# A two-layer decoder trunk on one core: the first norm's gain spread by TensorE from one row, the weight splits put behind the norm, the small S5 parameters moved by one block

## The chip, the cores and the metric

The kernel runs on one core of a Trainium2 chip. The metric is the device time of one execution in microseconds (us). In the text PE is TensorE, DVE VectorE, ACT ScalarE, POOL GpSimd, and SP the engine that issues most DMA transfers (SyncE).

## What is computed

256 tokens of width 1024 go through two layers. The part that matters here is the start of the first layer: a root-mean-square norm, then a gated feed-forward block.

```python
def rmsnorm(x, g):
    xf = x.astype(jnp.float32)
    y = xf * lax.rsqrt(jnp.mean(xf * xf, axis=-1, keepdims=True) + RMS_EPS)
    return (y * g.astype(jnp.float32)).astype(x.dtype)

def swiglu(x, w_gate, w_up, w_down):
    return (jax.nn.silu(x @ w_gate) * (x @ w_up)) @ w_down

for l in range(DEPTH):
    x = x + 0.5 * swiglu(rmsnorm(x, ffn1_norm[l]), ffn1_gate[l], ffn1_up[l], ffn1_down[l])
    ...
```

Behind it, in each layer, stand a mixer with three branches (sparse attention, an S5 state-space layer, dilated attention) and a second feed-forward block. The S5 layer needs tables that are made from its parameters (`s5_lam_re`, `s5_lam_im`, `s5_log_dt` and others). They are made while the first feed-forward block runs.

## The kernel before

Tokens stand in two tiles of 128, `x[0]` and `x[1]`. The weights arrive in units of 512 KB (`load_unit`, L210), four buffers deep (`raw`). Each unit is split in two: ACT copies it in a rounded form to `wh` (L221), and DVE makes the remainder `wl` (L228); in the first layer's feed-forward part DVE does nearly all of these remainders. Five pairs of `wh` and `wl` are held. A product of the kernel is three matmuls, high by high, high by low and low by high (`mm3`, L106 to L108), so a unit needs 24 matmuls of 256 columns in the gate and up parts. The hidden width of 2816 is worked off in blocks j of 256; a block takes two units for the gate and two for the up weights, and two for the down weights of block j-2.

The norm of a token tile (`norm_half`, L264, and `norm_tok`, L266 to L286) is a chain over the engines: ACT squares the two halves of the tile with a running sum, DVE adds the sums (L269), POOL raises to -1/2 (L271), DVE multiplies each half by that and by the gain (`xn`, L274), PE transposes it in four pieces (L278) into the PSUM tiles `y` and `p2`, ACT copies the result to the high part `hTh` (L282) and DVE makes the low part `hTl` (L283).

Before the first products PE runs 12 matmuls on zeros (`WARM`, L1147). The gain of the first norm is fetched by SP in two halves, each as one row of 2 KB read for all 128 partitions (L1150 and L1156), in between the loads of x[0] and of the first two weight units. So SP's first transfers are x[0], gain half, unit 0, gain half, unit 1, x[1], units 2 and 3, a table of masks (`cm`), and then the next units as their buffers come free.

The small parameters of the S5 layer are loaded in the feed-forward block's step j = 1 and worked on in step j = 2 (`step`, L1125 to L1138). They go by `setup_small`, which transposes `st_small` on PE into the PSUM tile `y` (L405) and copies it out on DVE (`smT`, L406), and by `setup_s5_params`, which transposes three more tiles into the same PSUM tile `y` (L438) and works on from there on DVE. `y` has one buffer, so L438 cannot start before L406 has read it.

The order of the instructions on each engine is set by a scheduler, which lays the program out by priorities and its own estimate of each operation's time. `tc.high_priority` raises a priority, and `tc.issue_after` (in `behind`, L288) makes an instruction stand behind another one.

Of the kernel before, what the change touches and what calls it, by code (L numbers as in the profile page):

```python
# [27 lines left out]
ALU = mybir.AluOpType  # L28
# [44 lines left out]
def _body(ctx, tc, nc, I, out, depth, dbg):  # L73
# [112 lines left out]
    WARM = 12  # L186
# [26 lines left out]
    def emit_unit(i):  # L213
        while pos[0] <= min(i + RB - 1, len(units) - 1):
            unit_t[pos[0]] = load_unit(pos[0])
            pos[0] += 1
        r = unit_t.pop(i)
        k, n = r.shape[1], r.shape[2]
        al, tags, nb = (tb, ("xh", "xl"), 4) if i in local else (sb, ("wh", "wl"), WB_)
        hv, lv = (al([P, 1024], F32R, tg, nb)[:, :k * n].rearrange("p (k c) -> p k c", k=k) for tg in tags)  # L220
        A.activation(hv, r, AF.Copy)  # L221
        if i in START or lo_share[0] and i % lo_share[1] < lo_share[0]:
            for c in range(0, n, n // 2):
                cs = slice(c, c + n // 2)
                G.tensor_tensor(lv[:, :, cs], r[:, :, cs], hv[:, :, cs].bitcast(F32), op=ALU.subtract)  # L225
        else:
            c = n - n * lo_share[2] // 8
            V.tensor_tensor(lv[:, :, :c], r[:, :, :c], hv[:, :, :c].bitcast(F32), op=ALU.subtract)  # L228
            if c < n:
                G.tensor_tensor(lv[:, :, c:], r[:, :, c:], hv[:, :, c:].bitcast(F32), op=ALU.subtract)  # L230
        unit_t[i] = (hv, lv)
# [33 lines left out]

    def norm_tok(t, g, h):  # L266
# [4 lines left out]
        G.tensor_tensor(rs, ms, mh[:, 0:1], op=ALU.pow)  # L271
        for q in range(2):
            xn = tb([P, 512], F32, "xn", 2)
            V.scalar_tensor_tensor(xn, x[t][:, q * 512:(q + 1) * 512], rs, g[:, q * 512:(q + 1) * 512],  # L274
                                   op0=ALU.mult, op1=ALU.mult)
            pt = ps(("y", "p2")[q])
# [5 lines left out]
            A.activation(hv, p3, AF.Copy)  # L282
# [842 lines left out]
    def step(gen, l):  # L1125
        def f(j):
# [4 lines left out]
            if j >= 2:  # L1131
                if l == 0 and j == 2:
# [7 lines left out]
    with Phase():  # L1140
        table(AF.Silu)
        with tc.high_priority():
# [3 lines left out]
            for _ in range(WARM):  # L1146
                PE.matmul(pw, wz[:, :P], wz, start=True, stop=True)  # L1147
            g = tb([P, D], F32, "G", 1)
            gs = I["ffn1_norm"][0].unsqueeze(0).broadcast_to([P, D])
            nc.sync.dma_start(g[:, :512], gs[:, :512])  # L1150
            for i in range(3):
# [3 lines left out]
                if i == 0:  # L1155
                    nc.sync.dma_start(g[:, 512:], gs[:, 512:])  # L1156
# [59 lines left out]
```

## Time and profile before

| | |
|---|---|
| runs | 1357.64, 1356.96 and 1354.83 us; median 1356.96 |
| the profiled execution | 1357.2 us |
| its span in the trace | 1355.4 us; 1.8 us lie around it |
| PE, share of the span | 98% |
| DVE, ACT, POOL | 61%, 52%, 34% |
| mean DMA rate | 196 GB/s |

A timeline row gives the start, the duration, the engine, the line, the operation, its output and inputs, how many equal ones follow, and in brackets for how long the engine had been idle and what ended that. Matmuls overlap on PE, so the step from one start to the next, not a matmul's own duration, is what it costs. A windows row gives the stretch, its length, the busy us (and the count of instructions) of PE, of PE's weight loads, of DVE, ACT and POOL, then the granted clock of PE (1.00 is 2.4 GHz, 0.50 is 1.2 GHz), the DMA share and GB/s.

### The profile page before, as it was taken

What the parts mean: (1) busy time and instruction counts of PE and PEld (TensorE: products, weight loads), DVE (VectorE), ACT (ScalarE), POOL (GpSimd) and SP (SyncE); (2) the same over time, 40 slices, a digit from 0 to 9 for tenths busy, and PEclk for the clock granted to TensorE, in tenths of its full rate; (3) what the DMA queues carried; (4) which work ended last, traced back from release to release, by engine and by line L of the source; (5) the groups of instructions that cost most, each with busy time, mean ns of one, the idle gap of its engine ahead of it and who ended that gap; (6) DMA issues with size and microseconds to landing.
All of it is one profiled execution on the core that took longest, in us unless ns stands there. A gap on an engine that the chain in (4) does not pass through costs nothing.

```text
span 1355.4 us, 25390 instructions
## 1 busy us (share of the span) xinstructions
PE 1331.6 (98%) x10120; PEld 1256.8 (93%) x10120; DVE 826.8 (61%) x1172; ACT 699.8 (52%) x1020; POOL 465.3 (34%) x333
## 2 busy tenths in 40 slices
PE   8999999999999999999999999999999999999998
PEld 7999988999999989999999999889999999899997
DVE  5696755996433665444675586569864337544443
ACT  5444445677644544444544444457766355544442
POOL 1442565454246531111122247254532555111110
PEclk9999999999999999999999999999999999999999
DMA  8866688666657556666756677766766576466662
GB/s 249 224 188 214 223 267 235 198 184 191 184 134 226 172 171 204 186 187 187 236 154 203 202 231 240 243 201 176 194 193 178 157 221 194 155 188 186 186 187 94
DMA packets 246326, 265.68 MB, mean 196 GB/s; under 512 B 51136, under 2 KB 224192, under 8 KB 246208
## 3 DMA queue, kind: packets, MB, share of 16 engines
q1 hardware_dynamic: 244400, 260.40, 64.7%
q10 hardware_dynamic: 1808, 3.67, 0.8%
q8 instruction: 79, 1.29, 0.4%
q14 instruction: 39, 0.32, 0.1%
HBM read 244.92 MB, written 18.58 MB: 194 GB/s over the span
## 4 chain that ended last, share of the span: by engine, by line
PE 76%; DVE 9%; DMA 7%; POOL 3%; ACT 2%; issue 2%; SPq 0%; ACTq 0%; DVEq 0%; POOLq 0%
PE mm L108 17%; PE mm L106 17%; PE mm L107 17%; PE pt L108 3%; PE pt L107 3%; PE pt L106 3%; DVE wl L228 3%; PE sc L108 3%; PE sc L107 3%; PE sc L106 3%; DMA raw<-in_w_in_dram 2%; DMA raw<-in_ffn_down_dram 1%; DMA raw<-in_ffn_gate_dram 1%; DMA raw<-in_ffn_up_dram 1%; PE pt L820 1%
## 5 line engine op out<-in xcount | busy, mean ns | idle before, releaser
L228 DVE TENSOR_TENSOR wl<-raw,wh 128x1024 fp32r<-128x1024 f32 (+3 forms) x376 | 443.5, 1186 | 340.8 <-ACT wh L221 327.2
L221 ACT ACTIVATE wh<-raw 128x1024 fp32r<-128x1024 f32 (+2 forms) x396 | 414.2, 1048 | 453.8 <-PE mm L107 240.8
L108 PE MATMUL mm<-hTh,wl 128*128 128x256 f32 x1728 | 490.7, 284 | 0.0
L107 PE MATMUL mm<-hTl,wh 128*128 128x256 f32 x1728 | 490.7, 284 | 0.0
L106 PE MATMUL mm<-hTh,wh 128*128 128x256 f32 x1728 | 489.0, 283 | 0.0
L106 PEld LDWEIGHTS mm<-hTh,wh 128*128 128x128 f32 x1728 | 326.5, 189 | 2.2
L108 PEld LDWEIGHTS mm<-hTh,wl 128*128 128x128 f32 x1728 | 325.9, 189 | 0.6 <-issue 0.3
L107 PEld LDWEIGHTS mm<-hTl,wh 128*128 128x128 f32 x1728 | 325.2, 188 | 1.3 <-issue 0.3
L371 POOL TENSOR_TENSOR al<-aa,ah 128x512 fp32r<-128x512 f32 x40 | 71.3, 1781 | 456.8 <-ACT ah L370 456.8
L230 POOL TENSOR_TENSOR wl<-raw,wh 128x384 fp32r<-128x384 f32 (+2 forms) x108 | 144.9, 1347 | 174.7 <-ACT wh L221 142.3
L106 PE MATMUL mm<-wh,hTh 128*128 128x256 f32 (+1 forms) x496 | 142.9, 290 | 0.0
L107 PE MATMUL mm<-wl,hTh 128*128 128x256 f32 (+1 forms) x496 | 141.8, 288 | 0.0
L108 PE MATMUL mm<-wh,hTl 128*128 128x256 f32 (+1 forms) x496 | 140.6, 288 | 0.0
L107 PEld LDWEIGHTS mm<-wl,hTh 128*128 128x128 f32 x496 | 94.1, 190 | 1.2 <-issue 0.3
L106 PEld LDWEIGHTS mm<-wh,hTh 128*128 128x128 f32 x496 | 94.0, 190 | 1.1 <-issue 0.3
L108 PEld LDWEIGHTS mm<-wh,hTl 128*128 128x128 f32 x496 | 93.1, 189 | 1.0 <-issue 0.3
L225 POOL TENSOR_TENSOR wl<-raw,wh 128x512 fp32r<-128x512 f32 x40 | 56.5, 1434 | 53.7 <-ACT wh L221 48.4
L107 PE MATMUL pt<-wl,ah 128*128 128x512 f32 x144 | 56.4, 392 | 0.0
L108 PE MATMUL pt<-wh,al 128*128 128x512 f32 x144 | 56.4, 391 | 0.0
L108 PE MATMUL sc<-wh,al 128*128 128x512 f32 x144 | 56.3, 391 | 0.0
L106 PE MATMUL pt<-wh,ah 128*128 128x512 f32 x144 | 56.2, 390 | 0.0
L107 PE MATMUL sc<-wl,ah 128*128 128x512 f32 x144 | 56.1, 390 | 0.0
(311 smaller groups left out, 2074.7 us busy)
## 6 DMA issues: line engine op xcount, KB each, us to landing
raw<-in_w_in_dram SPq DMA_DIRECT2D x100, 512.0 KB, 4.3
raw<-in_ffn_gate_dram SPq DMA_DIRECT2D x88, 512.0 KB, 4.4
raw<-in_ffn_up_dram SPq DMA_DIRECT2D x88, 512.0 KB, 4.7
raw<-in_ffn_down_dram SPq DMA_DIRECT2D x88, 512.0 KB, 4.3
raw<-in_w_out_dram SPq DMA_DIRECT2D x16, 512.0 KB, 4.2
Gd<-xh SPq DMA_DIRECT2D x8, 512.0 KB
Ad<-xl SPq DMA_DIRECT2D x8, 512.0 KB, 5.6
x<-Ad SPq DMA_DIRECT2D x8, 512.0 KB, 5.3
```

The lines of the kernel that those rows point to most:

```text
L106: PE.matmul(o, lh, rh, start=start, stop=False)
L107: PE.matmul(o, lh, rl, start=False, stop=False)
L108: PE.matmul(o, ll, rh, start=False, stop=stop)
L221: A.activation(hv, r, AF.Copy)
L225: G.tensor_tensor(lv[:, :, cs], r[:, :, cs], hv[:, :, cs].bitcast(F32), op=ALU.subtract)
L228: V.tensor_tensor(lv[:, :, :c], r[:, :, :c], hv[:, :, :c].bitcast(F32), op=ALU.subtract)
L230: G.tensor_tensor(lv[:, :, c:], r[:, :, c:], hv[:, :, c:].bitcast(F32), op=ALU.subtract)
L371: G.tensor_tensor(al, a, ah.bitcast(F32), op=ALU.subtract)
L820: PE.transpose(pt[:, i * P:(i + 1) * P], s[:, (b0 + i) * P:(b0 + i + 1) * P], ident)
```

## The change

Three things are done.

- The first norm's gain is fetched as one row of 4 KB to one partition, and two matmuls of that row with a column of ones spread it over 128 partitions in the PSUM tile `sc`. They stand between 7 and 5 of the zero matmuls. `xn` then reads the gain from PSUM.
- The split of unit 0 on DVE (`wl`) is put behind the last `xn` that was written (x[1]'s second half), and the split of unit 1 on ACT (`wh`) behind the last `hTh` (x[1]'s second). In `norm_tok` both `xn` are now written ahead of the transposes.
- The work on the small parameters moves from step j = 2 to j = 3.

```diff
-    WARM = 12
+    WARM = 7, 5
...
-        A.activation(hv, r, AF.Copy)
+        with behind(order.get("h") if i == 1 else None):
+            A.activation(hv, r, AF.Copy)
...
-            V.tensor_tensor(lv[:, :, :c], r[:, :, :c], hv[:, :, :c].bitcast(F32), op=ALU.subtract)
+            with behind(order.get("x") if i == 0 else None):
+                V.tensor_tensor(lv[:, :, :c], r[:, :, :c], hv[:, :, :c].bitcast(F32), op=ALU.subtract)
...
+        xns = []
         for q in range(2):
             xn = tb([P, 512], F32, "xn", 2)
-            V.scalar_tensor_tensor(xn, x[t][:, q * 512:(q + 1) * 512], rs, g[:, q * 512:(q + 1) * 512],
+            xns.append(xn)
+            order["x"] = V.scalar_tensor_tensor(xn, x[t][:, q * 512:(q + 1) * 512], rs, g[:, q * 512:(q + 1) * 512],
                                    op0=ALU.mult, op1=ALU.mult)
+        for q, xn in enumerate(xns):
...
-            A.activation(hv, p3, AF.Copy)
+            order["h"] = A.activation(hv, p3, AF.Copy)
...
-                if l == 0 and j == 2:
+                if l == 0 and j == 3:
...
-            for _ in range(WARM):
-                PE.matmul(pw, wz[:, :P], wz, start=True, stop=True)
-            g = tb([P, D], F32, "G", 1)
-            gs = I["ffn1_norm"][0].unsqueeze(0).broadcast_to([P, D])
-            nc.sync.dma_start(g[:, :512], gs[:, :512])
+            g1, one = tb([1, D], F32, "G1"), tb([1, P], F32, "one")
+            nc.sync.dma_start(g1, I["ffn1_norm"][0].unsqueeze(0))
+            V.memset(one, 1.0)
...
+            g = ps("sc")
+            w = warm(WARM[0])
+            for q in range(2):
+                with behind(w):
+                    w = PE.matmul(g[:, q * 512:(q + 1) * 512], one, g1[:, q * 512:(q + 1) * 512], start=True, stop=True)
+            with behind(w):
+                warm(WARM[1])
...
-                if i == 0:
-                    nc.sync.dma_start(g[:, 512:], gs[:, 512:])
```

**ACT at the start.** Of the names, `junk` are the squares of the norm, `x0` and `x1` the token tiles, `wh_48`, `wh_51` and so on the high parts of units 0, 1 and so on, and `hTh` the transposed norm's high part, twice for each token tile. Before:

```order
L264 ACTIVATE junk_23_122,n_ss_21_119<-x0_1_63 128x512
L221 ACTIVATE wh_48_187<-raw_18_111 128x1024
L282 ACTIVATE hTh_24_124<-y_29_132 128x4x128
L221 ACTIVATE wh_51_193<-raw_19_114 128x1024
L282 ACTIVATE hTh_24_124<-p2_31_141 128x4x128
L264 ACTIVATE junk_33_149,n_ss_32_148<-x1_2_64 128x512
L264 ACTIVATE junk_34_151,n_ss_32_148<-x1_2_64 128x512
L221 ACTIVATE wh_54_199<-raw_20_117 128x1024
L221 ACTIVATE wh_57_205<-raw_47_185 128x1024
L282 ACTIVATE hTh_24_124<-y_38_159 128x4x128
L245 DMA G_42_179<-in_mix_norm_dram 128x1024
L282 ACTIVATE hTh_24_124<-p2_40_168 128x4x128
L221 ACTIVATE wh_60_211<-raw_50_191 128x1024
```

and with the change, where units 0, 1, 2 and 3 are `wh_50`, `wh_53`, `wh_56` and `wh_59`:

```order
L266 ACTIVATE junk_25_126,n_ss_23_123<-x0_1_63 128x512
L222 ACTIVATE wh_50_191<-raw_20_116 128x1024
L266 ACTIVATE junk_35_153,n_ss_34_152<-x1_2_64 128x512
L289 ACTIVATE hTh_26_128<-y_32_138 128x4x128
L266 ACTIVATE junk_36_155,n_ss_34_152<-x1_2_64 128x512
L289 ACTIVATE hTh_26_128<-p2_33_145 128x4x128
L289 ACTIVATE hTh_26_128<-y_41_165 128x4x128
L247 DMA G_44_183<-in_mix_norm_dram 128x1024
L289 ACTIVATE hTh_26_128<-p2_42_172 128x4x128
L222 ACTIVATE wh_53_197<-raw_21_118 128x1024
L222 ACTIVATE wh_56_203<-raw_22_121 128x1024
L222 ACTIVATE wh_59_209<-raw_49_189 128x1024
```

Now x1's first square stands between unit 0 and the first `hTh` of x0, and units 1 and on stand behind all four `hTh`.

**DVE at the start.** `wl_49` and `wl_52` are the low parts of units 0 and 1. Before:

```order
L274 SCALAR_TENSOR_TENSOR xn_28_130<-x0_1_63,n_rs_27_128,G_17_109 128x512
L274 SCALAR_TENSOR_TENSOR xn_30_139<-x0_1_63,n_rs_27_128,G_17_109 128x512
L228 TENSOR_TENSOR wl_49_188<-raw_18_111,wh_48_187 128x1024
L283 TENSOR_TENSOR hTl_25_125<-y_29_132,hTh_24_124 128x4x128
L228 TENSOR_TENSOR wl_52_194<-raw_19_114,wh_51_193 128x1024
L283 TENSOR_TENSOR hTl_25_125<-p2_31_141,hTh_24_124 128x4x128
L269 TENSOR_SCALAR n_ms_35_153<-n_ss_32_148 128x1
L274 SCALAR_TENSOR_TENSOR xn_37_157<-x1_2_64,n_rs_36_155,G_17_109 128x512
L274 SCALAR_TENSOR_TENSOR xn_39_166<-x1_2_64,n_rs_36_155,G_17_109 128x512
L228 TENSOR_TENSOR wl_55_200<-raw_20_117,wh_54_199 128x1024
L408 TENSOR_TENSOR sgn_10_78<-cm_3_66 128x1 x2
L228 TENSOR_TENSOR wl_58_206<-raw_47_185,wh_57_205 128x1024
```

and with the change, where they are `wl_51` and `wl_54`:

```order
L280 SCALAR_TENSOR_TENSOR xn_30_134<-x0_1_63,n_rs_29_132,sc_19_101 128x512
L280 SCALAR_TENSOR_TENSOR xn_31_136<-x0_1_63,n_rs_29_132,sc_19_101 128x512
L290 TENSOR_TENSOR hTl_27_129<-y_32_138,hTh_26_128 128x4x128
L273 TENSOR_SCALAR n_ms_37_157<-n_ss_34_152 128x1
L290 TENSOR_TENSOR hTl_27_129<-p2_33_145,hTh_26_128 128x4x128
L280 SCALAR_TENSOR_TENSOR xn_39_161<-x1_2_64,n_rs_38_159,sc_19_101 128x512
L280 SCALAR_TENSOR_TENSOR xn_40_163<-x1_2_64,n_rs_38_159,sc_19_101 128x512
L230 TENSOR_TENSOR wl_51_192<-raw_20_116,wh_50_191 128x1024
L415 TENSOR_TENSOR sgn_10_78<-cm_3_66 128x1 x2
L290 TENSOR_TENSOR hTl_27_129<-y_41_165,hTh_26_128 128x4x128
L436 MEMSET sp_eb_153_850 128x64
L290 TENSOR_TENSOR hTl_27_129<-p2_42_172,hTh_26_128 128x4x128
L230 TENSOR_TENSOR wl_54_198<-raw_21_118,wh_53_197 128x1024
```

Unit 0's low part has gone from behind x0's `xn` to behind x1's, unit 1's behind the last `hTl`; the gain now comes from the PSUM tile `sc`.

**PE at the start, with the change.** After x0's transposes PE has one product, then x1's transposes, then eleven more products of unit 0 with x0, of which the last are here:

```order
L108 MATMUL mm_70_231<-wh_50_191,hTl_27_129 128x256
L106 MATMUL mm_70_231<-wh_50_191,hTh_26_128 128x256
L107 MATMUL mm_70_231<-wl_51_192,hTh_26_128 128x256
L108 MATMUL mm_70_231<-wh_50_191,hTl_27_129 128x256
L106 MATMUL mm_70_231<-wh_53_197,hTh_26_128 128x256
L106 MATMUL mm_71_232<-wh_56_203,hTh_26_128 128x256
L107 MATMUL mm_70_231<-wl_54_198,hTh_26_128 128x256
```

The products that follow unit 0's need unit 1's high part (`wh_53`), unit 2's (`wh_56`) and unit 1's low part (`wl_54`); the last row is the fifteenth product. Before, 25 products stood ahead of x1's transposes.

**DVE around the small parameters.** `smT` is the copy for which PE's second set of transposes waits. Before, `wl_102` and `wl_105` are the low parts of units 11 and 12:

```order
L228 TENSOR_TENSOR wl_91_439<-raw_79_344,wh_90_438 128x1024
L228 TENSOR_TENSOR wl_102_494<-raw_82_374,wh_101_493 128x1024
L369 TENSOR_TENSOR aa_77_342<-mm_85_405,silu_76_341 128x512
L228 TENSOR_TENSOR wl_105_524<-raw_86_406,wh_104_523 128x1024
L406 COPY smT_11_79<-y_119_652 128x8
L409 TENSOR_TENSOR gqk_12_80<-smT_11_79 128x2
L410 TENSOR_TENSOR gqk_12_80<-smT_11_79 128x2
```

and with the change, where `wl_120`, `wl_135` and `wl_138` are those of units 16, 17 and 18:

```order
L376 TENSOR_TENSOR aa_100_493<-mm_108_556,silu_99_492 128x512
L230 TENSOR_TENSOR wl_120_629<-raw_109_557,wh_119_628 128x1024
L230 TENSOR_TENSOR wl_135_685<-raw_112_587,wh_134_684 128x1024
L230 TENSOR_TENSOR wl_138_715<-raw_115_620,wh_137_714 128x1024
L413 COPY smT_11_79<-y_152_843 128x8
L416 TENSOR_TENSOR gqk_12_80<-smT_11_79 128x2
```

The copy has moved by one block of weights; in both orders it stands right behind the low part of a block's first down unit. A part of the mixer in the second layer stands in another order too; the rest of the program stands as before.

## Rows read from the trace of the kernel before

**Rows 1.** The page: the span, and busy time by engine.

```profile
span 1355.4 us, 25390 instructions
PE 1331.6 (98%) x10120; PEld 1256.8 (93%) x10120; DVE 826.8 (61%) x1172; ACT 699.8 (52%) x1020; POOL 465.3 (34%) x333
```

**Rows 2.** Waits of PE, whole span: for what, us in total, times, longest.

```profile
PE y L278 <- DVE xn L274: 4.0, 4, 1.1
...
PE y L438 <- DVE smT L406: 1.8, 1, 1.8
```

**Rows 3.** Timeline of PE: start, us, engine, line, operation, out<-in, count, idle before.

```profile
1.18 5.30 PE L1147 MATMUL mm<-warm 128*128 128x512 bf16 x12 [1.18 <-DVE mh L252]
...
10.59 0.56 PE L106 MATMUL mm<-wh,hTh 128*128 128x256 f32 x1
...
17.31 0.28 PE L108 MATMUL mm<-wh,hTl 128*128 128x256 f32 x1
...
18.03 0.28 PE L108 MATMUL mm<-wh,hTl 128*128 128x256 f32 x1
```

**Rows 4.** Windows: first products alone (PE, PEld, DVE, ACT), then all instructions.

```profile
10.58:17.30 6.72, 5.56 (x28) 4.71 (x29) 0.00 (x0) 0.00 (x0) 0.77 1.07 354
...
10.20:13.60 3.40, 3.38 (x15) 2.83 (x14) 3.29 (x5) 2.91 (x7) 0.00 (x0) 0.50 1.08 359
...
365.20:368.60 3.40, 3.40 (x18) 3.40 (x18) 1.19 (x3) 1.77 (x5) 0.00 (x0) 0.50 1.01 268
```

**Rows 5.** Timeline of ACT, first 18 us.

```profile
4.19 0.63 ACT L264 ACTIVATE junk<-x 128x512 bf16<-128x512 f32 x1 [1.50 <-DMA x<-in_x_dram]
...
10.65 1.06 ACT L221 ACTIVATE wh<-raw 128x1024 fp32r<-128x1024 f32 x1 [0.66 <-DMA raw<-in_ffn_gate_dram]
...
12.10 0.62 ACT L264 ACTIVATE junk<-x 128x512 bf16<-128x512 f32 x1
...
12.84 0.63 ACT L264 ACTIVATE junk<-x 128x512 bf16<-128x512 f32 x1
...
16.70 0.60 ACT L282 ACTIVATE hTh<-p 128x512 fp32r<-128x512 f32 x1
...
17.39 1.06 ACT L221 ACTIVATE wh<-raw 128x1024 fp32r<-128x1024 f32 x1
```

**Rows 6.** Timeline of DVE, 13 to 20 us.

```profile
13.60 0.22 DVE L269 TENSOR_SCALAR n_ms<-n_ss 128x1 f32<-128x1 f32 x1
...
14.48 1.42 DVE L274 SCALAR_TENSOR_TENSOR xn<-x,n_rs,G 128x512 f32<-128x512 f32 x2 [0.67 <-POOL n_rs L271]
...
15.81 1.22 DVE L228 TENSOR_TENSOR wl<-raw,wh 128x1024 fp32r<-128x1024 f32 x1
...
18.84 0.68 DVE L283 TENSOR_TENSOR hTl<-p,hTh 128x512 fp32r<-128x512 f32 x1
```

**Rows 7.** Windows of the start; the last two columns are DMA share and GB/s.

```profile
0.00:4.00 4.00, 2.82 (x7) 1.04 (x8) 0.30 (x2) 1.89 (x4) 0.69 (x6) 1.00 0.52 154
4.00:7.00 3.00, 2.48 (x6) 0.60 (x4) 0.43 (x2) 1.44 (x4) 0.56 (x1) 1.00 0.84 216
7.00:9.20 2.20, 0.66 (x4) 0.42 (x4) 0.57 (x2) 0.74 (x1) 0.00 (x0) 1.00 1.05 378
```

**Rows 8.** Timelines of SP, PE, ACT and DVE around 43 us, by time.

```profile
35.63 1.38 SPq L210 DMA_DIRECT2D raw<-in_ffn_down_dram  x1
...
40.24 0.22 PE L405 MATMUL y<-ident,st_small 8*128 8x8 f32 x1
...
42.54 1.06 ACT L221 ACTIVATE wh<-raw 128x1024 fp32r<-128x1024 f32 x1 [2.27 <-DMA raw<-in_ffn_down_dram]
...
43.63 1.23 DVE L228 TENSOR_TENSOR wl<-raw,wh 128x1024 fp32r<-128x1024 f32 x1 [1.50 <-ACT wh L221]
...
44.77 0.16 DVE L406 COPY smT<-y 128x8 f32<-128x8 f32 x1
...
44.99 0.34 PE L438 MATMUL y<-ident,sp_raw 64*128 64x64 f32 x2 [1.84 <-DVE smT L406]
```

More of the change, by code (lines that the diff above doesn't have):

```diff
@@ L264, in norm_half @@
         A.activation(jk, x[t][:, q * 512:(q + 1) * 512], AF.Square, scale=1.0 / 32, accum_out=ssq[t][:, q:q + 1])
+    order = {}
     def norm_tok(t, g, h):
@@ L1145, in _body, with warm @@
             pw = ps("mm")
-            for _ in range(WARM):
-                PE.matmul(pw, wz[:, :P], wz, start=True, stop=True)
-            g = tb([P, D], F32, "G", 1)
-            gs = I["ffn1_norm"][0].unsqueeze(0).broadcast_to([P, D])
-            nc.sync.dma_start(g[:, :512], gs[:, :512])
+            g1, one = tb([1, D], F32, "G1"), tb([1, P], F32, "one")
+            nc.sync.dma_start(g1, I["ffn1_norm"][0].unsqueeze(0))
+            V.memset(one, 1.0)
+            def warm(n):
+                for _ in range(n):
+                    w = PE.matmul(pw, wz[:, :P], wz, start=True, stop=True)
+                return w
+            g = ps("sc")
[5 more added lines that the diff above has]
+                warm(WARM[1])
             for i in range(3):
```

## The prediction, made before the changed kernel was run

> **What bounds the kernel now.** The page comes first [rows 1]: PE is busy for 1331.6 of 1355.4 us, DVE for 61%, ACT for 52%. With PE at 98% the time is PE's work plus the moments in which PE waits or runs at half clock, so a change can only win or lose those. The waits of PE are the second view [rows 2]: four waits for a norm's `xn`, 4.0 us together, and one of 1.8 us for `smT`, the copy of the small parameters. The timelines of PE, ACT and DVE at the start come third [rows 3, 5, 6], since two of the three edits lie there. Last are the rows around 43 us [rows 8], where the third edit lies.
>
> At the start, read how far PE has come once the norm of both token tiles is behind it. From 17.31 us on PE starts a product every 0.12 us (six steps to 18.03 [rows 3]). By 17.30 it has done 28 products since 10.59 [rows 3, 4], the first of them at half clock (0.50 from 10.2 to 13.6 [rows 4]). 28 x 0.12 = 3.4 us, so PE stands where it would stand had it begun at 13.9 us without a pause. That number is what the change has to beat.
>
> **The start, first half: when x[1] lands.** The gain's two broadcast halves (0.52 MB written) go, and a row of 4 KB comes. With the change ACT's order is unit 0's split, the first square of x1, only then the first `hTh` of x0. So everything behind hangs on the landing of x1, L. Before, 2.10 MB went ahead of x1: x0, two gain halves, two units. The windows add up to 4.0 x 154 + 3.0 x 216 + 2.2 x 378 = 2.10 MB by 9.2 us [rows 7], and the last of these, unit 1, is taken up by ACT at 10.65 [rows 5], 1.4 us later. Now 2.10 MB is the whole of x0, units 0 and 1, and x1 itself. At the old rates x1 lands at 9.2 + 1.4 = 10.6: the upper bound. The lower one takes the slow stretch from 4 to 7 us (216 GB/s) as the gain's doing: 0.62 MB are over by 4.0, the other 1.48 MB go at 378, so at 7.9, and x0's delay is added (its 0.52 MB are through at 3.4 by the first of these rates, and ACT takes it up at 4.19 [rows 5]): 8.7. Nothing before tells these apart; I take about the middle, **L = 9.5**.
>
> **The start, second half: the chain from L.** First square at L; to the next ACT instruction 0.74 (12.10 to 12.84 [rows 5]); one `hTh` of 0.60 [rows 5] in between; second square at L + 1.34. Its `hTh` follows at +0.74 and takes 0.60, so L + 2.68; DVE makes `hTl` from it, 0.68 [rows 6], until L + 3.36. POOL's root is ready by then (from square to `n_ms` 0.76, to `xn` 0.88 more: L + 2.98 [rows 5, 6]). Two `xn`: 1.33 (14.48 to 15.81 [rows 6]). Unit 0's low part runs from L + 4.7 to L + 5.9. Until then PE has one product and x1's transposes; the next eleven need that low part. Then come the two `hTl` of x1, 0.6 each, a small `sgn`, and unit 1's low part of 1.22 [rows 6]: ready at L + 8.4. ACT's side (`hTh` to L + 6.1, units 1 and 2 at 1.06 each [rows 5], to L + 8.2) ends just before. The fifteenth product needs unit 1's low part, so 14 x 0.12 = 1.7 us of work stand ahead of L + 8.4, whether they ran at half clock (11 at half of a zero matmul's 0.44 us [rows 3], 2.4 us, fit between L + 5.9 and L + 8.4) or not. PE's equivalent start is L + 6.7 = **16.2 us, 2.3 later than before**; with the bounds of L 15.4 to 17.3, so 1.5 to 3.4 later. From there on a split is ready before PE comes to it: a unit costs DVE 1.22 and PE 24 x 0.12 = 2.9.
>
> Spreading the gain is priced at nothing: the row lands soon behind x0, and the two matmuls need to end by about 6.8, when DVE took its first `xn` before; the zero matmuls, also 512 wide, take 5.30/12 = 0.44 each [rows 3], so seven end at 4.3 and two spreads at 5.5 if they cost as much. The slack behind is the time to the first `hTh`, due at L + 0.74 = 10.2. Reading the gain from PSUM costs nothing either: `hTl`, which reads PSUM, takes 0.68, an `xn` 0.71 [rows 6]. Bounds: nothing, and half a us if the spreads take so long that the first `hTh` misses its turn (a rival, below).
>
> **Small parameters.** PE transposes `st_small` at 40.24, and the next set starts at 44.99 after 1.84 us of idle PE [rows 8], so 2.9 us of products lie in between. `smT` stood on DVE behind unit 12's low part (43.63), that behind ACT's split (42.54), that behind a load issued at 35.63 which took 6.9 us [rows 8], in the midst of the S5 loads. One block on, `smT` stands behind unit 18, whose load is issued after all S5 loads, with about as many products on PE between the two sets of transposes. I take the whole wait as gone, **-1.84 us**; the bounds are 0 and -1.84. The work behind it has a block less until the tables are used; DVE is busy for 61% of the span [rows 1], and I price that at nothing.
>
> **Sum.** 1357.2 (the profiled execution, 0.2 above the median of the runs) + 2.3 - 1.8 + 0.0 = **1357.7 us**. Two things have no sign and stand in the range: the rearranged piece of the second layer's mixer, and stretches of half clock such as 365.2 to 368.6 us, in which PE did 18 instructions without a wait [rows 4]; one of them costs 3.4/2 = 1.7 us, and may vanish or appear when PE's work shifts by 2 us.
>
> **Rivals.**
> - *The wait for `smT` is moved, not removed* (slower). It decides at DVE's copy behind unit 18's low part: if that ends over 2.9 us after `st_small`'s transpose, PE stands again. For it speaks that the copy again follows a block's first down unit; against it that loads are then no longer held up by small ones. 1357.2 + 2.3 = 1359.5.
> - *Units 10 and 11 come late* (slower). SP now has nearly all S5 loads ahead of unit 10's, where before they stood behind it. Unit 12's load was issued at 35.63 behind some of them; if unit 10's now goes out at 36, with 6.9 us to landing and 1.06 + 1.23 us for the splits [rows 8], it is ready at 45.2; PE wants unit 10 at 16.2 + 240 x 0.12 = 45.0, and some tenths later for the transposes in between. It is a draw; if SP is 1.5 us later, 1.5 us of wait: 1359.2.
> - *x1 lands early and a half-clock stretch goes* (faster): 1357.2 + 1.5 - 1.84 - 1.7 = 1355.2. For it speaks that the slow stretch of loads [rows 7] coincides with the gain; against it that nothing shows what starts the later half-clock stretch.
> - *The spreads are dear* (within no change). A zero matmul of 512 columns costs 0.44 us [rows 3], 1.2 columns a ns, so half clock, though the clock column of the windows says 1.00 there [rows 7]; I go by the step. If a spread costs four of them, 1.8 us, then two end at 4.3 + 3.6 = 7.9, the five zero matmuls at 10.1, and x0's first transposes and their `hTh` come 0.5 us after the 10.2 at which ACT would take it: 1358.2. For it speaks that the operands are plain FP32; against it that at full clock all of this is twice as fast. The Trainium skill, FP8 and Floating Point Precision, section TensorE Precision Notes, says that a true FP32 matmul makes four passes through the array; no row of this trace has a full-width one to show it; by the zero matmuls' row the sum stays at 1357.7, by four passes it is 1358.2.
> - *The gain's broadcast was not what held the loads*, so the first edit does not do what it is for: L = 10.6, 1357.2 + 3.4 - 1.84 = 1358.8.
>
> **How the numbers follow.** The forecast has 0.45, the dear spreads 0.12, the moved wait 0.10, late units 0.11, the early landing 0.12, the late landing 0.10. The time is the likeliest case's, 1357.7. The low end is the early case, 1355.2, the high end the late landing with 1.5 us of waits, 1360.3; 0.5 us are added at either end for the scatter of the runs (1354.8 to 1357.6). A measurement of this kernel can tell about 0.2%, 2.7 us, from no change, so faster means below 1354.2 and slower above 1359.7. All cases' own values lie between; of the early case and of an unforeseen gain in the mixer 0.10 falls below, of the slower ones 0.18 above: 0.10, 0.72 and 0.18.
>
> **What would show it.** Right: x1's first square on ACT near 9.5, products dense from about 15.4, the fifteenth near 17.9, no PE wait for `smT`, and an otherwise unchanged list of waits. Wrong: x1 before 8.7 or after 10.6; dense products before 14; a PE wait for a split between 40 and 50 us or for `smT` near 62; a gain that comes from the mixer.

## The result and the profile after

The changed kernel is slower: 1365.51 us, the median of 7 runs (1361.97 to 1369.22), against 1356.55 (1352.96 to 1357.64) on the same chip. The ratio is 1.0067, with a 95% interval of 1.0049 to 1.0084, so about 9 us are lost where 1357.7 us, no change, was forecast. The profiled execution, 1361.97 us, is the fastest of the seven. Ratios, here and below, leave out three executions (one each of b_j3, c_ld and the kernel before) that took over 2000 us; medians do not.

The page and the list of PE's waits answer to [rows 1, 2]:

```profile
span 1360.2 us, 25401 instructions
...
PE 1335.6 (98%) x10124; PEld 1259.2 (93%) x10124; DVE 828.6 (61%) x1173; ACT 699.7 (51%) x1020; POOL 464.5 (34%) x333
```

```profile
PE y L285 <- DVE xn L280: 4.8, 4, 2.0
...
PE y L368 <- DVE aa L364: 2.2, 1, 2.2
...
PE pt L107 <- DVE wl L230: 1.0, 1, 1.0
```

The wait for `smT` is gone, as forecast. Two new ones have come: one for `aa` and one for a low part `wl`. (`aa` is the first block's product of gate and up, made by DVE from `silu`; PE transposes it before the block's down matmuls.) The timeline of PE at the start, beside [rows 3]:

```profile
1.18 3.17 PE L1159 MATMUL mm<-warm 128*128 128x512 bf16 x7 [1.18 <-DVE warm L1151]
4.28 3.77 PE L1165 MATMUL sc<-G,one 1*128 1x512 f32 x4
...
11.84 0.58 PE L106 MATMUL mm<-wh,hTh 128*128 128x256 f32 x1
14.41 1.09 PE L285 MATMUL y<-ident,xn 128*128 128x128 f32 x4 [1.99 <-DVE xn L280]
...
16.11 0.58 PE L107 MATMUL mm<-wl,hTh 128*128 128x256 f32 x1
...
19.30 0.52 PE L107 MATMUL mm<-wl,hTh 128*128 128x256 f32 x1
...
20.04 0.28 PE L107 MATMUL mm<-wl,hTh 128*128 128x256 f32 x1
```

One product is done by 16 us, where the kernel before did most of its 28 [rows 4]; up to 19.8 the step is 0.21 us, half clock, and from 20.04 on 0.12. ACT's timeline, beside [rows 5], holds x1's landing and the first `silu`, which comes 3.26 us later than in the kernel before (the first fence):

```profile
23.51 0.66 ACT L356 ACTIVATE silu<-mm 128x256 f32<-128x256 f32 x2 [0.86 <-PE mm L108]
```

```profile
10.45 0.63 ACT L266 ACTIVATE junk<-x 128x512 bf16<-128x512 f32 x1 [1.71 <-DMA x<-in_x_dram]
...
26.77 0.66 ACT L363 ACTIVATE silu<-mm 128x256 f32<-128x256 f32 x2 [0.67 <-PE mm L108]
```

The `silu` is a poor mark of the start, since fewer products stand ahead of it now (75 in the records, 81 before). A better one is the end of the first block: its 96 products are over where the first product of the next block stands, which has its operands the other way round (`mm<-hTh,wh`). Before, then after:

```profile
25.47 0.28 PE L106 MATMUL mm<-hTh,wh 128*128 128x256 f32 x1
```

```profile
29.41 0.28 PE L106 MATMUL mm<-hTh,wh 128*128 128x256 f32 x1
```

So PE is 3.94 us late when the first block is done. DVE's timeline, beside [rows 6]:

```profile
14.83 1.22 DVE L230 TENSOR_TENSOR wl<-raw,wh 128x1024 fp32r<-128x1024 f32 x1
...
17.96 3.50 DVE L230 TENSOR_TENSOR wl<-raw,wh 128x1024 fp32r<-128x1024 f32 x3 [0.26 <-ACT wh L222]
...
32.27 0.15 DVE L439 TENSOR_SCALAR sp_cor<-sp_ld 64x1 f32<-64x1 f32 x1 [4.92 <-DMA sp_ld<-in_s_log_dt_dram]
...
35.57 0.74 DVE L364 TENSOR_TENSOR aa<-mm,silu 128x256 f32<-128x256 f32 x2
```

The low parts of units 0 to 3 start between 14.83 and 20.3 us; before, they started between 9.84 and 17.09. And `aa`, whose `silu` was done at 27.4, stands behind `sp_cor` on DVE's row, which idles 4.92 us for the transfer of `s_log_dt`. Before, `aa` stood ahead of it:

```profile
26.29 0.75 DVE L357 TENSOR_TENSOR aa<-mm,silu 128x256 f32<-128x256 f32 x2
...
31.74 0.15 DVE L432 TENSOR_SCALAR sp_cor<-sp_ld 64x1 f32<-64x1 f32 x1 [2.05 <-DMA sp_ld<-in_s_log_dt_dram]
```

Next, the loads on SP. The first fence is the kernel before, where units 4 and 5 go out at 11.09 and unit 10 at 28.32. The second is the changed kernel: units 2 and 3 at 3.09, unit 4 only at 16.12, units 5 to 8 from 21.38 to 24.57, unit 10 at 37.59.

```profile
11.09 2.28 SPq L210 DMA_DIRECT2D raw<-in_ffn_gate_dram  x2
...
28.32 0.54 SPq L210 DMA_DIRECT2D raw<-in_ffn_up_dram  x1
```

```profile
3.09 1.45 SPq L210 DMA_DIRECT2D raw<-in_ffn_up_dram  x2
...
16.12 0.37 SPq L210 DMA_DIRECT2D raw<-in_ffn_gate_dram  x1
...
21.38 0.39 SPq L210 DMA_DIRECT2D raw<-in_ffn_gate_dram  x1
...
24.57 1.03 SPq L210 DMA_DIRECT2D raw<-in_ffn_gate_dram  x1
...
26.84 0.60 SPq L431 DMA_DIRECT2D sp_ld<-in_s_log_dt_dram  x1
...
37.59 0.40 SPq L210 DMA_DIRECT2D raw<-in_ffn_up_dram  x1
```

SP's waits from 5 to 45 us (for what, us in total, times, longest; before, then after) say what held these loads: the one at 16.12 waited 9.4 us for the low part that frees its buffer, unit 0's, which ends at 16.05.

```profile
SPq L210 <- DVE wl L228: 4.9, 4, 2.6
```

```profile
SPq L210 <- DVE wl L230: 9.6, 2, 9.4
```

Windows of all engines (the last two columns are DMA share and GB/s), first the kernel before, then the changed one:

```profile
10.00:25.00 15.00, 14.92 (x105) 13.83 (x106) 11.09 (x16) 9.69 (x15) 0.97 (x2) 0.89 0.96 316
25.00:35.00 10.00, 10.00 (x87) 10.00 (x86) 6.72 (x11) 5.01 (x7) 1.62 (x1) 1.00 0.68 139
```

```profile
10.00:25.00 15.00, 13.01 (x76) 12.05 (x75) 10.24 (x15) 7.51 (x12) 0.97 (x2) 1.00 0.57 184
25.00:35.00 10.00, 8.85 (x75) 8.64 (x73) 3.37 (x6) 4.90 (x6) 0.54 (x1) 1.00 1.04 206
...
37.50:40.90 3.40, 3.40 (x20) 3.40 (x19) 1.83 (x2) 0.59 (x2) 0.00 (x0) 0.56 1.16 224
```

In the changed kernel the DMA engines are half idle from 10 to 25 us, (316 - 184) x 15 us = 2.0 MB or nearly four units behind, and full from 25 to 35. (The 1.00 in the clock column of its first row does not fit the steps of 0.21 us up to 19.8, which say half clock; the text goes by the steps.)

In this execution: 3.94 us at the start, 2.19 for `aa`, 1.7 for the half-clock stretch behind that wait (3.4 us at half speed, last row), 1.0 for `wl`, less 1.84 for `smT`: 7.0. The first update of x at the end of the first network came at 216.5 us instead of 208.8, 7.7 later; the other 0.7 lie in no wait of the list. The two mixers gave about 2.1 each back, in the second one mostly because the half-clock stretch that the kernel before had there (at 1034 us, worth 1.7 us) was absent, and at the end the span is 4.8 us longer. The gain in the second mixer does not repeat: another execution of the changed kernel did not have it (a_again, below).

### The profile page after: what moved, and what is told of

The parts are those of the page before. It is cut to its first block, busy times and chain, and to the rows that moved or that the text cites. A ratio compares the mean times of both kernels' runs of the same rounds, so it can differ in the third digit from the quotient of the medians.

```text
span 1360.2 us, 25401 instructions
## 1 busy us (share of the span) xinstructions
PE 1335.6 (98%) x10124; PEld 1259.2 (93%) x10124; DVE 828.6 (61%) x1173; ACT 699.7 (51%) x1020; POOL 464.5 (34%) x333
## 4 chain that ended last, share of the span: by engine, by line
PE 73%; DVE 11%; DMA 5%; POOL 4%; issue 3%; ACT 3%; SPq 1%; POOLq 0%; ACTq 0%; DVEq 0%
PE mm L106 17%; PE mm L108 17%; PE mm L107 17%; DVE wl L230 4%; PE pt L107 3%; PE pt L108 3%; PE pt L106 3%; PE sc L108 2%; PE sc L107 2%; PE sc L106 2%; DMA raw<-in_w_in_dram 2%; DMA raw<-in_ffn_gate_dram 1%; ACT wh L222 1%; PE pt L827 1%; PE y L953 1%
```

## The experiments

Ratios are to the kernel before on the same chip. "Rate" is the DMA rate from 10 to 25 us, "silu" the start of the first `silu`, "x" the first update of x, each in the profiled execution.

| run | what it is | median us | ratio (95%) | rate | silu | x |
|---|---|---|---|---|---|---|
| before | | 1356.55 | | 316 | 23.51 | 208.8 |
| after | all three edits | 1365.51 | 1.0067 (1.0049 to 1.0084) | 184 | 26.77 | 216.5 |
| a_again | the same again | 1366.29 | 1.0070 (1.0047 to 1.0092) | 169 | 26.30 | 217.1 |
| a_noord | without the two orders | 1357.99 | 1.0006 (0.9991 to 1.0020) | 266 | 25.52 | 209.8 |
| a_nospread | without the spread | 1362.90 | 1.0054 (1.0035 to 1.0074) | 199 | 27.36 | 218.7 |
| a_j2 | parameters at block 2 | 1364.54 | 1.0066 (1.0045 to 1.0088) | 167 | 27.14 | 214.7 |
| a_cor | `sp_cor` behind `aa` | 1369.27 | 1.0101 (1.0079 to 1.0124) | 176 | 26.55 | 218.3 |
| a_xx | order on DVE alone | 1361.52 | 1.0041 (1.0027 to 1.0055) | 211 | 26.38 | 212.1 |
| a_hx | order on ACT alone | 1361.17 | 1.0039 (1.0024 to 1.0054) | 204 | 25.70 | 214.0 |
| a_x0 | orders behind x0's norm | 1358.39 | 1.0012 (0.9998 to 1.0025) | 268 | 24.96 | 208.9 |
| c_raw2 | a_cor, two more buffers | 1366.64 | 1.0078 (1.0052 to 1.0103) | 214 | 28.73 | 216.2 |
| a_raw2 | after, two more buffers | 1367.20 | 1.0070 (1.0045 to 1.0095) | 219 | 28.83 | 216.1 |
| c_ld | c_raw2, loads in order | 1362.82 | 1.0031 (1.0014 to 1.0049) | 257 | 26.73 | 214.2 |
| a_ld | a_raw2, loads in order | 1360.04 | 1.0028 (1.0014 to 1.0041) | 263 | 26.89 | 212.1 |
| b_raw2 | before, two more buffers | 1361.07 | 1.0028 (1.0011 to 1.0045) | 316 | 22.62 | 214.6 |
| b_hold | before, loads held | 1358.94 | 1.0013 (1.0000 to 1.0026) | 245 | 24.65 | 210.4 |
| b_spread | the spread alone | 1356.02 | 0.9995 (0.9981 to 1.0010) | 260 | 24.07 | 208.3 |
| b_j3 | the parameters alone | 1357.37 | 1.0003 (0.9989 to 1.0016) | 318 | 23.70 | 207.8 |
| b_split | `smT` alone to block 3 | 1355.01 | 0.9988 (0.9972 to 1.0004) | 296 | 24.74 | 209.8 |
| bs_split | spread and b_split | 1356.52 | 0.9990 (0.9976 to 1.0004) | 264 | 24.14 | 208.5 |

### Which edit loses

The first four took one edit away each, or the new wait.

**a_noord.** Both `behind(order.get(...))` become `behind(None)`:

```
-        with behind(order.get("h") if i == 1 else None):
+        with behind(None):
...
-            with behind(order.get("x") if i == 0 else None):
+            with behind(None):
```

> The changed kernel without its two orders (low part of unit 0 behind xn, high part of unit 1 behind hTh); spread and moved parameters stay. Theory A (the orders changed DVE's row so that `sp_cor` came ahead of `aa`; without them `aa` stands ahead of it again): no wait of PE for `aa`, no half-clock stretch at 37.5, 3 to 4 us faster than the changed kernel; the start stays late, with the first square of x1 at 10.3 to 10.6 and full clock only from 19 to 20.5 us, so 0.5 to 3 us slower than the kernel before. Theory B (the spread's late start makes `aa` late): as the changed kernel, within 1 us. If the orders helped the start at all, the fifteenth product comes later than 19.3 us here.

Measured 1.0006: the orders carry the loss. PE waits for nothing between 15 and 75 us. The spread and the moved parameters together can't be told from no change. The start is not wholly mended: the first block ends at 27.46, 2.0 us later than in the kernel before, of 3.9.

**a_nospread.** The broadcast transfers and `WARM = 12` return; orders and parameters stay.

> The changed kernel without the spread: the factors come by the broadcast transfers as before, with twelve zero matmuls; orders and moved parameters stay. Theory A (the start is late by the spread's PE time of two times 1.9 us, and by the clock that stays at half until about 20 us; `aa` however is set by the landing of `s_log_dt` at about 32 us and not by PE): the clock is full from about 14 us, the first silu comes at 23 to 24.5 us instead of 26.8, but the wait for `aa` grows by what the start gains, to 3.5 to 5.5 us, with a half-clock stretch behind it; the whole is within 0 to 1.5 us of the changed kernel. Theory B (waits add up, each with its own price): 3 us faster than the changed kernel with the wait for `aa` at about 2.2.

Measured 1.0054: the loss is there without the spread. The wait for `aa` was 3.6 us, as A said, but the start was not early: `silu` at 27.36, no earlier than with the spread. x1 landed at 12.04 here and 10.45 with the spread, and the orders hold the products until x1's norm is through (PE waits 4.0 us for its `xn`). So theory A had the late start in the wrong edit: it comes for the most part from the orders.

**a_j2.** `j == 3` becomes `j == 2`.

> The changed kernel with the small S5 parameters back at block 2; spread and orders stay. Theory A (the move saves the wait for `smT`, 1.84 us, but puts the S5 table work on POOL beside low parts on DVE at 99 to 111 us, which cost 3.0 and 3.4 us instead of 1.2 and made PE wait 1.0 us for `wl`): the wait for `smT` is back with 1 to 2 us, the wait for `wl` is gone, `aa` still waits about 2 us, and the time is 0 to 1.5 us above the changed kernel's. Theory B (it is the moved parameters that put `sp_cor` ahead of `aa`): the wait for `aa` and the half-clock stretch go, 2 to 3 us faster than the changed kernel.

1.0066: the move makes no difference in this kernel. The wait for `wl` went, as A said; that for `smT` did not come back; `aa` waited 1.4 us, and 1.2 us for a `silu` were new.

**a_cor.** The new wait taken out of the way:

```
+                            order["a"] = V.tensor_tensor(a[:, t], ...
...
+        with behind(order.get("a")):
+            V.tensor_scalar(cor, ld, le, 1.0, op0=ALU.mult, op1=ALU.add)
```

> The changed kernel with one added order: on DVE the correction of the S5 step sizes (`sp_cor`, which waits for the transfer of `s_log_dt`) stands behind the first block's products `aa`; nothing is computed otherwise. Theory A (DVE's queue: `aa` waited behind `sp_cor`, its two small followers and two low parts, PE stood 2.19 us at 33.9 to 36.0 us and then ran at half clock from 37.5 to 40.9): `aa` starts at 32 to 34 us, the wait of `y L368` falls from 2.19 to under 0.9, the half-clock stretch behind it is gone, and the run is 1.5 to 3.9 us faster than the changed kernel (of 1361.97 us profiled, 1365.5 median: 1358 to 1360.5 profiled). Theory B (the late start alone is to blame, `aa` is late because everything before it is): the wait stays at about 2 us and the time at 1362 to 1365.5.

Both theories fell: the wait for `aa` went and the kernel lost no less, 1.0101. PE now stood at 40 us (waits, then ACT's timeline):

```profile
PE mm L106 <- ACT silu L374: 4.2, 1, 4.2
```

```profile
37.62 1.06 ACT L222 ACTIVATE wh<-raw 128x1024 fp32r<-128x1024 f32 x1 [5.18 <-DMA raw<-in_ffn_gate_dram]
...
43.82 1.06 ACT L222 ACTIVATE wh<-raw 128x1024 fp32r<-128x1024 f32 x1 [4.66 <-DMA raw<-in_ffn_up_dram]
44.78 0.58 ACT L374 ACTIVATE silu<-mm 128x512 f32<-128x512 f32 x1
```

ACT's row was stopped by a unit's data, and `silu` stood behind it. The wait for `aa` was where a shortage showed, not what made it. From here theory L says that the orders hold the raw buffers and so the loads.

### How much order, how much loss

**a_xx** keeps only the order on DVE, **a_hx** only that on ACT, **a_x0** both, but behind x0's norm (`order["x", 0]`, `order["h", 0]`).

> The changed kernel with the order on DVE alone (low part of unit 0 behind the last xn); the high part of unit 1 is free. Theory L (the orders hold the raw buffers: the four buffers are freed only by the low parts, so the loads of the next units start late, the DMA engines moved 184 GB/s instead of 316 between 10 and 25 us, and the time lost is PE standing at 30 to 45 us for units that come late): low parts 0 to 2 end at 16 to 19 us instead of 16 to 21.5, the DMA rate in 10:25 is between 200 and 270 GB/s, the first down and up units come earlier, and the time lies between the changed kernel (1365.5) and it without orders (1358): 1360 to 1363.5. Theory S (the loss is the start of the products, which wait for x1's norm): the start is as late as in the changed kernel, so is the time, 1364 to 1366.

> The changed kernel with the order on ACT alone (high part of unit 1 behind the last hTh); the low part of unit 0 is free. Theory L (loads held by the raw buffers): buffer 0 is freed at about 9 to 10 us, but buffers 1 to 3 only at 19 to 22 us, the DMA rate in 10:25 stays at 190 to 240 GB/s, and the time is 1361 to 1365, nearer to the changed kernel than to it without orders. Theory S (the loss is the start of the products): the products of unit 0 start at 12 to 13 us, before x1's norm, and some 15 of them are done by 16 us, so that two thirds of the loss go: 1358.5 to 1360.5.

> The changed kernel with both orders set behind the norm of x0 alone (low part of unit 0 behind xn of x0, high part of unit 1 behind hTh of x0). Low part 0 then ends at about 10.8 us, the low parts 1 to 3 at 16 to 19. Theory L: loads go on at 240 to 290 GB/s in 10:25, no wait for `aa` or for silu at 30 to 45 us, and the time is within 2 us of the changed kernel without orders (1358), which is 7 us faster than the changed kernel. Rival (any order behind the norm is dear, since the queue of ACT or DVE is stopped): 1362 to 1365.

All three fall into the ranges of L. With less held, the rate rises (184, then 204 and 211, then 268 GB/s) and the ratio falls (1.0067, then 1.0039 and 1.0041, then 1.0012). In a_hx the products started early and it lost no less than a_xx. But the start improves in the same order: the first block ends at 29.41 in the changed kernel, at 28.79 in a_xx, 28.34 in a_hx and 25.95 in a_x0. In a_xx PE waits for nothing from 15 to 75 us, and its first update of x is 3.3 us late, just as its first block is. So these three fit held loads and a late start alike; the runs that send the loads early (below) tell them apart.

**b_hold** holds the loads alone, in the kernel before:

```
+        if i in (4, 5):
+            with behind(order["x"] if i == 4 else order["l"]):
+                V.memset(r[0:1, 0, 0:1], 0.0)
         nc.sync.dma_start(r, src)
```

> The kernel before, with the loads alone held: the raw tiles of units 4 and 5 get one element written by DVE behind x1's xn and behind x1's last hTl, so that these two loads, and what stands behind them on SP, go out at about 16 and 19.5 us instead of 11.1; no order on ACT's splits or DVE's low parts, no spread. Theory L: the DMA rate in 10:25 falls from 316 to 180 to 250 GB/s, units 4 to 10 come 3 to 6 us later, PE stands for data between 25 and 45 us, and the time is 2 to 6 us above the kernel before. Theory Q: within 1 us of the kernel before.

1.0013, 1.8 us, with an interval that begins at 1.0000: a little under the range of L. The rate fell only to 245, near a_x0 and a_noord, and those lose as little. The stop that L names did not come: unit 4 went out at 16.20 and unit 10 at 33.90, over 5 us later than in the kernel before, but PE waited for no unit from 15 to 75 us. So held loads alone, at this rate, are not shown to cost anything.

### The loads sent early, the orders kept

**c_raw2, a_raw2 and b_raw2** give units 3 and 4 raw tiles of their own:

```
-        r = sb([P, 1024], F32, "raw", RB)...
+        r = (tb([P, 1024], F32, "raw2", 2) if i in (3, 4) else sb([P, 1024], F32, "raw", RB))...
...
-        while pos[0] <= min(i + RB - 1, len(units) - 1):
+        while pos[0] <= min(i + RB + (1 if i < 4 else -1), len(units) - 1):
```

> The kernel of the run a_cor (the changed kernel with `sp_cor` behind `aa`; 1369.3 us, PE stood 4.2 us at 40 us because ACT waited 5.2 us for a unit's data) with two more buffers for raw units: units 3 and 4 load into two tiles of their own, so that two more loads need no buffer to come free; rows of DVE and ACT stay as they are. Theory L (the orders held the raw buffers, the loads came late): the DMA rate in 10:25 goes from 176 to over 250 GB/s, the waits at 37 to 45 us go, and the time falls by 5 to 10 us, to 1359 to 1364; what is left is the late start of the products (about 3 us). Theory Q (the order of the rows on DVE and ACT holds the products, not the data): the time stays at 1366 to 1372.

> The changed kernel itself with the same two more buffers; `aa` still stands behind `sp_cor` on DVE. Theory L: the DMA rate in 10:25 goes from 184 to over 250 GB/s and units 5 to 10 come earlier; but `sp_cor` waits for `s_log_dt`, whose transfer stands behind more unit loads in SP's queue now, so the wait for `aa` stays (2 to 6 us) and takes back part: 1360 to 1366, above c_raw2 in any case. Theory Q: as the changed kernel, 1364 to 1367, and as c_raw2.

> The kernel before with the same two more buffers and nothing of the change. In the kernel before the DMA engines are busy in 10:25 (0.96) and PE waits for nothing but `smT` between 15 and 75 us, so more buffers bring nothing by theory L: within 2 us of the kernel before. Where `smT` moves on DVE's row, its wait of 1.84 us may go or grow. Rival (the loads bound the kernel before too): 3 to 5 us faster.

c_raw2 and a_raw2 say little of L, since they did not do what they were for. The loads of units 3, 4 and 5 now needed no buffer to come free, but SP's row put two of the three behind the load that waits for low part 0 (c_raw2):

```profile
3.57 0.55 SPq L210 DMA_DIRECT2D raw<-in_ffn_gate_dram  x1
...
16.37 0.92 SPq L210 DMA_DIRECT2D raw<-in_ffn_up_dram  x2
```

The rate rose to 214 and 219 only. In a_raw2 no wait for `aa` showed, though 2 to 6 us were expected; PE waited for high parts, a `silu` and a low part (1.5, 1.3 and 0.6 us). b_raw2 was a miss: its new row had 76 GB/s from 25 to 35 us and `aa` behind `sp_cor`, and it lost 3.8 us.

**c_ld and a_ld** add that SP sends the units in their order:

```
+        with behind(order.get("ld")):
+            order["ld"] = nc.sync.dma_start(r, src)
```

> The kernel of the run c_raw2 with SP's loads of units kept in the order of the units, so that the loads of units 3, 4 and 5 go out at once, and only unit 6 waits for low part 0. Theory L: the DMA rate in 10:25 is above 240 GB/s, units 3 to 5 are split without waiting for data, and the time falls to 1359 to 1363 (from 1366.6 for c_raw2 and 1369.3 for a_cor). Theory Q (rows of ACT and DVE): 1365 to 1370 with the DMA rate up.

> The changed kernel with the two more buffers and SP's loads in the order of the units, as in c_ld, but with `aa` behind `sp_cor` as in the changed kernel. If only the held loads cost (theory L), it comes to 1361 to 1364, as c_ld (1362.8), with little or no wait for `aa`. If the place of `aa` costs by itself, PE waits 2 to 6 us for `aa`, since `s_log_dt` still lands at 30 to 33 us and PE ends the first block at 31 to 33, and the time is 1364 to 1368.

a_ld is the changed kernel, orders and all, with `aa` still behind `sp_cor`; its loads alone go out early (SP's timeline, then windows, DVE's timeline and PE's waits from 15 to 75 us):

```profile
4.51 0.37 SPq L212 DMA_DIRECT2D raw<-in_ffn_up_dram  x1
...
4.93 2.70 SPq L212 DMA_DIRECT2D raw<-in_ffn_gate_dram  x2
16.36 0.37 SPq L212 DMA_DIRECT2D raw<-in_ffn_up_dram  x1
...
25.43 0.60 SPq L432 DMA_DIRECT2D sp_ld<-in_s_log_dt_dram  x1
```

```profile
10.00:25.00 15.00, 12.87 (x75) 11.83 (x74) 11.36 (x16) 8.14 (x13) 0.97 (x2) 1.00 0.81 263
25.00:35.00 10.00, 10.00 (x87) 10.00 (x86) 5.87 (x10) 4.99 (x7) 0.54 (x1) 1.00 0.77 142
```

```profile
27.75 0.15 DVE L440 TENSOR_SCALAR sp_cor<-sp_ld 64x1 f32<-64x1 f32 x1 [2.70 <-DMA sp_ld<-in_s_log_dt_dram]
...
31.05 0.74 DVE L365 TENSOR_TENSOR aa<-mm,silu 128x256 f32<-128x256 f32 x2
```

```profile
PE y L286 <- DVE xn L281: 2.1, 1, 2.1
```

The products start as late as in the changed kernel (`silu` at 26.89, the first block's end at 29.54), but behind that PE is not short of a split up to 75 us. `s_log_dt` lands 2.3 us after its issue and not 5.4 (in the changed kernel four unit loads went out just ahead of it, from 21.38 to 24.57); so `aa` is in time, in the same place on DVE's row. The ratio falls from 1.0067 to 1.0028, and from 1.0101 to 1.0031 for c_ld. a_raw2 and a_ld differ in SP's order alone, and their intervals (1.0045 to 1.0095, 1.0014 to 1.0041) lie apart. The place of `aa` costs nothing that shows once the loads are on time. That is L, at 1360.0 a little under its range.

a_ld's ACT row also shows why its start is as late, though x1 landed 0.76 us earlier than in the changed kernel:

```profile
9.69 0.63 ACT L268 ACTIVATE junk<-x 128x512 bf16<-128x512 f32 x1 [2.67 <-DMA x<-in_x_dram]
...
11.27 0.60 ACT L290 ACTIVATE hTh<-y 128x512 fp32r<-128x512 f32 x1 [0.86 <-PE y L286]
```

The first `hTh` waited for x0's transposes on PE, which stand behind the two spreads and the five zero matmuls; x1's second square stands behind that `hTh`.

### The scatter, and the other two edits

> The changed kernel once more. A second profile: the wait for `aa` is there again (1.4 to 4 us), with the first silu at 26 to 28 us; median 1363 to 1367. If the scatter of its runs comes from TensorE's clock, the profile shows another number of half-clock stretches than the first one (three inside the run) or a start at full clock; if from the loads, another landing time of `s_log_dt` or of the units at 30 to 45 us.

1.0070, the same again. The second profile has the same chain with a longer stop: 3.00 us for `aa`, and 6.8 us at half clock instead of 3.4 (its window):

```profile
35.50:42.30 6.80, 5.98 (x28) 5.98 (x29) 4.05 (x6) 1.54 (x2) 0.00 (x0) 0.51 1.13 243
```

PE is busy for 5.98 of the 6.8, so 3.0 + 3.0 stand against 2.2 + 1.7, 2.1 us more. But the first block ended 0.5 us earlier (28.89), and at the first update of x this execution is only 0.6 behind the other. Of the 3.6 us by which its span is longer 3.1 come in the second layer's mixer, where from the first update of x ahead of it (882.9) to the first behind it (1165.1) 282.2 us pass instead of 279.1 (281.4 in the kernel before). So the stop and the clock behind it explain little of the scatter of 7 us.

> The kernel before with the spread alone (factors by PE from one row, 7 and 5 zero matmuls, the two scalings of a token ahead of its transposes), parameters at block 2, no orders. x1's first square at 10.4 to 10.7 us as in every kernel with the spread; the spreads take 2.0 us together where TensorE is at full clock, 3.8 where it is at half; first silu 1.5 to 2.5 us later than in the kernel before; the time 0 to 3 us above the kernel before: 1357 to 1360.5. Rival of the record (the broadcast held the loads, so that the spread brings x1 earlier): 1354 to 1356.

0.9995, below what was expected. The late landing of x1 (10.66) is there, but `silu` is only 0.56 us late and the first block's end 0.54 (26.01), and no time is lost that could be measured.

> The kernel before with the small S5 parameters at block 3 instead of block 2, nothing else. As forecast, the wait of PE for `smT` (1.84 us) goes; the wait for `wl` of 1.0 us at about 110 us, seen in every kernel with the moved parameters and in none with them at block 2, comes in its place. Sum: 0.5 to 1.5 us faster than the kernel before, within 0.2 per cent of it. Rival (the move also makes the loads of the next blocks earlier): 2 to 4 us faster. Rival (the S5 work collides more with the low parts): 0 to 2 us slower.

1.0003. By the profile the terms are right: x is updated at 207.8 instead of 208.8, -1.84 for `smT` and +1.0 for `wl`. In the changed kernel the latter looks like this (timeline of all engines): beside POOL's work for the S5 tables, now a block later, a low part takes 3.41 us instead of 1.22, and PE waits for it.

```profile
107.35 3.38 POOL L593 TENSOR_TENSOR xh<-xh,xl 128x1024 f32<-128x1024 f32 x1
...
108.39 3.41 DVE L230 TENSOR_TENSOR wl<-raw,wh 128x1024 fp32r<-128x1024 f32 x1
...
111.86 0.50 PE L107 MATMUL pt<-wl,ah 128*128 128x512 f32 x1 [0.96 <-DVE wl L230]
```

**b_split** moves only the transposed rows (`smT`, `gqk`) to block 3, by a second `yield` in `setup_small` and

```
-                if l == 0 and j == 2:
+                if l == 0 and j in (2, 3):
...
-                        for a in small:
+                        for a in small[:j == 2 and 2 or 1]:
```

> The kernel before, with only the transposed norm rows (`smT`, `gqk`) moved to block 3; the S5 parameters and the sign stay at block 2. PE's transposes of the S5 parameters then find no `smT` ahead of them in the shared tile `y`: the wait of 1.84 us goes, and the S5 tables stay where they were, so that the wait of 1.0 us for `wl` at 110 us doesn't come. The end of the first network comes 1.5 to 2 us earlier than in the kernel before (first update of x at 206.8 to 207.3 instead of 208.8), the time 1 to 2 us below the kernel before, within 0.2 per cent. Rival (as with all parameters moved): no gain, 1357 to 1358.

Both waits are gone, and the ratio is 0.9988, with an interval that reaches 1.0004. The update of x came at 209.8, not at 207: a longer half-clock stretch at the start (6.8 us from 10.6) made `silu` 1.2 us late in that execution. **bs_split** puts the spread to it:

> The kernel before with the spread, without the orders, and with only the transposed norm rows (`smT`, `gqk`) moved to block 3. The spread alone was 1.3 us below the kernel before and the move alone 2.3, neither told from no change. If both add up: 1353 to 1355, 2 to 4 us faster than the kernel before. If these were scatter and only the wait for `smT` counts: 1355 to 1357. No wait of PE for `smT`, none for `aa`, none for `wl` at 110 us.

0.9990 (0.9976 to 1.0004): the gains don't add up. No version here beats the kernel before by more than can be told.

## Why the prediction was wrong

- **The step that failed** is the sentence that closes the start: "From there on a split is ready before PE comes to it: a unit costs DVE 1.22 and PE 24 x 0.12 = 2.9." It prices a split by the engine that makes it and forgets that a low part is also what frees a raw buffer, and so what lets the next load go: unit 4's load waited 9.4 us for unit 0's low part. The sum should have carried a term for it. a_ld, where only the loads are sent early, is 0.39% below the changed kernel, 5.3 us of the 9.1 lost. With it falls "an otherwise unchanged list of waits".
- **The late start** was right in kind and too small. Counted as the prediction counts, 96 products of 0.12 us back from the first block's end (29.41), PE stands as if it had begun at 17.9, 4.0 us behind 13.9; the sum had 2.3, at most 3.4. x1 landed at 10.45 and not at 9.5, the fifteenth product came 8.85 us behind that and not 8.4, and half clock lasted beyond it, until 20.04. (With the landing as it came L + 6.7 is 17.15, 3.25 us behind 13.9, and the first `silu` is 3.26 late. That they agree is luck, since fewer products stand ahead of this `silu` than before.)
- **The landing** was not what decided. In the fourteen profiles with the spread, whose SP rows are the same up to x1's load, x1 landed between 9.36 and 10.86, so that L = 9.5 and the 10.6 of the rival both occur. With the broadcast it landed at 12.04 (a_nospread), but fewer bytes go ahead of it without, which the rival has in its 10.6 too; whether the broadcast also slowed the other loads is not shown. And where x1 landed before 9.8 (a_j2, a_xx, a_x0, c_raw2, c_ld, a_ld) its second square came at 11.69 to 12.13, no earlier than the 11.68 of the changed kernel, as the first `hTh` waited for x0's transposes.
- **The spreads** cost what the rival of dear spreads said: 3.77 us for two, ending at 8.05 with the five zero matmuls at 10.30, and the first `hTh` came at 11.19 and not at 10.2. (The 5.5 at which two spreads as cheap as zero matmuls were to end should read 5.2 by the same rows, which changes nothing.) In a_cor they took 2.01 us at full clock (below). The Trainium skill, FP8 and Floating Point Precision, section TensorE Precision Notes, gives four passes for true FP32; by that rule, the traces agree: 1.9 us each beside 0.44 for a zero matmul at half clock. Priced at nothing, they were wrong beside the orders, where they hold the start even when x1 lands early; without the orders they cost no time that shows (b_spread, 0.9995).
- **The small parameters** were right in the -1.84 and wrong in the nothing for the rest: 1.0 us came back as a wait for `wl` beside POOL (b_j3).
- **The rival of late units** had the right place and the wrong cause. It put unit 10's load at 36 because of the S5 loads ahead of it; it went out at 37.59, but units 4 to 9 were late already, because of the buffers.
- What the order of the instructions could have told beforehand: `aa` behind `sp_cor`. It would have been the wrong lesson, since moving it back lost no less.
- **Not settled**: by its ratio a_ld still loses 3.8 us (1.9 to 5.6). The start (4.1), `wl` (1.0) and `smT` (-1.8) make 3.3, and its first update of x, at 212.1, is 3.2 us late, so the late start would account for it. But the two more buffers alone lost as much in the kernel before (b_raw2), and no run has them with SP's order and without the orders on ACT and DVE. What makes some runs of the changed kernel 5 us slower than others is open.

## What to carry to other kernels

Where an instruction that reads a ring of load buffers is put behind something, ask when the buffers come free, not only when its result is needed: here four buffers held at 10 us were paid for at 35. When a new wait shows, take it out alone before believing it; if the time does not fall, it was the place where a shortage came to light. And an experiment on loads must be read in the row of the queue that issues them.

## What was not expected of the hardware

- The clock at the start differs between executions of one program. The spreads took 3.77 us in the first profile of the changed kernel and 2.02 in the second (a_again); 3.75 in a_ld and b_spread, and about half of that in a_noord (1.95) and a_cor (its PE timeline):

```profile
4.46 2.01 PE L1166 MATMUL sc<-G,one 1*128 1x512 f32 x4
```

- Half clock around and behind a stop of PE: 3.4 us with a stop of 2.2 us, 6.8 with one of 3.0 (a_again), 3.4 with one of 4.2 (a_cor). Its length does not follow the stop's.
- A low part on DVE takes 3.41 us instead of 1.22 while POOL works on tiles of the same size.
